# Where the split weight tiles of a two-layer encoder start inside their SBUF buffers

## The chip, the cores and the metric

One Trainium2 chip; the program runs on one of its cores. The metric is device microseconds of one execution of the whole program, and the time of a kernel is the median of several executions. One further execution is taken with the profiler on, and all rows below come from that one.

## What is computed

Two transformer layers on 256 tokens of width 1024, in float32. Each layer is a SwiGLU block, a mixer with three attention branches that share one input projection, and a second SwiGLU block. Cut to what matters here:

```python
for l in range(DEPTH):                                   # DEPTH = 2, D_MODEL = 1024, D_FF = 2816
    x = x + 0.5 * swiglu(rmsnorm(x, norm_ffn1[l]), w_ffn1_in[l], w_ffn1_out[l])
    h = rmsnorm(x, norm_mix[l])
    qa, ka, va, qb_, kb, vb, qc, kc, vc, gate_logits = jnp.split(h @ w_in[l], split_points, axis=-1)
    y_a, y_b, y_c = mixer_a(...), mixer_b(...), mixer_c(...)
    branches = jnp.einsum('bsnw,nwd->bsnd', jnp.stack([y_a, y_b, y_c], axis=2), w_branch[l])
    gates = jax.nn.sigmoid(gate_logits.reshape(b, s, N_BRANCH, D_MODEL))
    x = x + jnp.sum(gates * branches, axis=2) @ w_out[l]
    x = x + 0.5 * swiglu(rmsnorm(x, norm_ffn2[l]), w_ffn2_in[l], w_ffn2_out[l])
return rmsnorm(x, norm_final)
```

The weights are 215 MB in float32 and each is read once.

## The kernel before

Every weight matrix is cut into chunks of one MB, 2048 float32 in each of 128 partitions, and all chunks stand in one list, `specs`, in the order of use (196 of them). `ahead` keeps the list moving: it issues the load of a chunk to a `raw` buffer from SP, and `split` makes two tiles of it. The **upper part** `hi` is the chunk rounded to the type fp32r (L284, a cast on ScalarE), the **lower part** `lo` is the rest, raw minus hi (L285, a subtraction on VectorE, or on GpSimd for 25 chunks). Each of the two instructions covers half a chunk, 1024 elements. `raw`, `hi` and `lo` have a pool each with three buffers (`wraw`, `whi`, `wlo`), so the chunks take buffers 0, 1, 2, 0, 1, 2 in turn.

Activations are split in the same way. A product is then three matmuls into one PSUM bank, by `mm3` (L301 to L303): upper weights by upper activations, upper weights by lower activations, lower weights by upper activations. In `mm3` a 128x128 piece of `hi` or `lo` is the stationary operand, loaded anew for each matmul, and 256 tokens of the activations are the moving one. TensorE is written by hand and runs these loads and matmuls in program order, so that a stage is a long run of pairs of one load and one matmul. The names in the rows are those of the PSUM tiles that are written:

- `gu`: the gate and up projections of a SwiGLU block, moving operand `xgh`, `xgl` (the normalised input, 8 slices of 256 tokens), 4224 matmuls in four blocks.
- `fm`: the mixers' input projections, the same moving operand, 1920 matmuls.
- `facc`: the SwiGLU output projection of three of the four blocks, moving operand `hh`, `hl`, 1584 matmuls.
- `br`: the three branch projections of the mixers, moving operand `yah` to `ycl`, 576 matmuls.
- `wacc`: the mixers' output projection, moving operand `mh`, `ml`, 384 matmuls.

Two places use the weights as moving operand, 512 wide: `facc` of the last block (L382 to L384, 264 matmuls) and `vps`, the attention values (L874 to L876, 96 matmuls). The rest of TensorE's work (`sc`, `pt`, `o`, `oc` and small ones, attention) does not touch `hi` or `lo`.

The tiles' places in SBUF are fixed when the program is built. Before the change all three `hi` buffers and all three `lo` buffers start at the same place in a span of 512 bytes: byte 256 (their addresses are 69376, 77568, 85760 and 93952, 102144, 110336). A 128-column piece of weights is 512 bytes long and starts at a multiple of 512 bytes in its tile, so that every stationary operand starts at byte 256 of such a span too. The moving operands of `facc`, `br` and `wacc` also start at byte 256; those of `gu` and `fm`, `xgh` and `xgl`, start at byte 448.

Of the kernel before, what the change touches and what calls it, by code (L numbers as in the profile page):

```python
# [12 lines left out]
F32R = mybir.dt.float32r  # L13
# [4 lines left out]
P = 128  # L18
# [53 lines left out]
def encoder(ctx: ExitStack, tc: tile.TileContext, a, rope, onehot, out):  # L72
# [3 lines left out]
    whi = ctx.enter_context(tc.tile_pool(name="whi", bufs=3))  # L76
    wlo = ctx.enter_context(tc.tile_pool(name="wlo", bufs=3))
# [10 lines left out]
    def f(ap):  # L88
        return ap.bitcast(F32)
# [171 lines left out]
    raws, parts = [], []  # L261

    def ahead(n_raw, n_split):
        while len(raws) < min(n_raw, len(specs)):
            srcs, shape, _ = specs[len(raws)]
            raw = wraw.tile([P] + shape, F32, tag="raw", name="raw")
            for sl, ap in srcs:
                nc.sync.dma_start(out=raw if sl is None else raw[sl], in_=ap)
            raws.append(raw)
        while len(parts) < min(n_split, len(specs)):  # L270
            for _ in split(2):
                pass

    def split(n, eng=None):

        _, shape, pool_lo = specs[len(parts)]
        raw = raws[len(parts)]
        hi = whi.tile([P] + shape, F32R, tag="hi", name="hi")
        lo = wlo.tile([P] + shape, F32R, tag="lo", name="lo")
        parts.append((hi, lo))  # L280
        n = shape[0] // n
        for i in range(0, shape[0], n):
            h = slice(i, i + n)
            nc.scalar.copy(out=hi[:, h], in_=raw[:, h])  # L284
            (eng or (nc.gpsimd if pool_lo else nc.vector)).tensor_sub(lo[:, h], raw[:, h], f(hi[:, h]))  # L285
            yield
# [648 lines left out]
    with tc.manual_schedule(engines=BY_HAND):  # L935
        gains(rows, 2 * KT, 0)
        sst = sm.tile([P, 2], F32, name="sst", bufs=1)
        state["sst1"] = sm.tile([P, 2], F32, name="sst1", bufs=1)
        xps = [bank(acc, "ps_x") for _ in range(4)]
        for tt in range(2):  # L940
            for m in range(KT):
                nc.tensor.transpose(xps[m // 2][:, m % 2, cs(tt)], xtok[:, tt, cs(m)], ident)
        first = split(4, nc.gpsimd)
        for b in range(4):
            for i in range(2):
                m = 2 * b + i
                nc.scalar.activation(out=xgh[:, m, :], in_=xps[b][:, i, :], func=AF.Identity, scale=gcol[:, m:m + 1])
            nc.vector.tensor_copy(out=xT[:, 2 * b:2 * b + 2, :], in_=xps[b])
            for i in range(2):
                scaled_lo(2 * b + i, 0)  # L950
            next(first)
        for _ in first:
            pass
        for tt in range(2):
            for i in range(2):
                junk = t2("junk").rearrange("p a s -> p (a s)")
                acc_to = sst if i == 0 else state["sst1"]
                nc.scalar.activation(out=junk, in_=xtok[:, tt, i * 512:(i + 1) * 512], func=AF.Square, accum_out=acc_to[:, tt:tt + 1])
        nc.vector.tensor_add(sst, sst, state["sst1"])
        state["sst"] = sst  # L960
# [36 lines left out]
```

## Time and profile before

| | |
|---|---|
| median of 3 executions | 1248.13 us (1247.22 to 1248.27) |
| profiled execution | 1248.98 us, of which the span from the first to the last instruction is 1247.2 us |
| TensorE, matmuls | 1199.9 us busy, 96% of the span, 9720 matmuls |
| TensorE, weight loads | 1175.2 us, 94%, 9720 loads |
| VectorE, ScalarE, GpSimd | 812.0, 679.4 and 391.5 us busy (65%, 54%, 31%) |
| mean granted clock of TensorE | 0.987 of full speed |

How to read it: a matmul's row lasts some 280 ns, but the next one starts some 115 ns after it, since they are pipelined and their ends are modelled. What a stretch of TensorE costs is therefore read from the starts of its matmuls, or from their count in a stretch that is busy throughout, not from the duration of one. [...]

### The profile page before, as it was taken

To read this page: it belongs to the slowest core of one execution; us is meant where nothing else is said; L and a number is where in the kernel's file an instruction comes from. 1 tells how busy PE (TensorE), PEld (TensorE's weight loads), DVE (VectorE), ACT (ScalarE), POOL (GpSimd) and SP (SyncE) were. 2 spreads that over 40 slices of the span, in tenths; PEclk is the share of its full clock that TensorE was granted. 3 is DMA by queue.
4 is the path that set the end of the run, shared out by engine and by line. 5 is a ranking of instruction groups with operands and counts; after the bars stand their busy time and mean duration, and the time that the engine had idled before them with its cause. 6 is when DMAs were issued, how large, how long until landed. Compare 5 with 4: busy or idle time off the path is not lost. (4 is left out here: it accounts for less than half of the span.)

```text
span 1247.2 us, 23166 instructions
## 1 busy us (share of the span) xinstructions
PE 1199.9 (96%) x9720; PEld 1175.2 (94%) x9720; DVE 812.0 (65%) x1090; ACT 679.4 (54%) x1117; POOL 391.5 (31%) x244
## 2 busy tenths in 40 slices
PE   7999999998999999999999999998999999999997
PEld 6999999898999999999999999987988999999996
DVE  5565557777778675555575555587688867655554
ACT  5444445488875564434463443455988665444443
POOL 2221215643343232222242222274443613222221
PEclk9999999999999999999999999998999999999999
DMA  7658664344445456655555555544444445555550
GB/s 255 208 200 289 211 200 148 124 160 132 133 154 177 152 189 200 198 176 200 178 195 182 191 197 178 191 137 142 137 154 151 136 168 170 204 171 198 175 200 34
DMA packets 169365, 218.16 MB, mean 175 GB/s; under 512 B 4302, under 2 KB 147200, under 8 KB 169260
## 3 DMA queue, kind: packets, MB, share of 16 engines
q1 hardware_dynamic: 168652, 215.09, 51.8%
q8 instruction: 76, 1.25, 0.4%
q10 hardware_dynamic: 464, 1.06, 0.2%
q0 software_dynamic: 144, 0.52, 0.1%
q14 instruction: 29, 0.24, 0.1%
HBM read 215.59 MB, written 4.22 MB: 176 GB/s over the span
## 5 line engine op out<-in xcount | busy, mean ns | idle before, releaser
L284 ACT CAST hi<-raw 128x1024 fp32r<-128x1024 f32 (+1 forms) x394 | 399.1, 1043 | 413.4 <-issue 356.2
L285 DVE TENSOR_TENSOR lo<-raw,hi 128x1024 fp32r<-128x1024 f32 x342 | 455.1, 1357 | 134.0 <-ACT hi L284 133.2
L302 PE MATMUL gu<-xgl,hi 128*128 128x256 f32 x1408 | 393.1, 279 | 4.8 <-DVE xgl L316 4.8
L301 PE MATMUL gu<-xgh,hi 128*128 128x256 f32 x1408 | 393.6, 280 | 0.2 <-ACT hi L284 0.2
L303 PE MATMUL gu<-xgh,lo 128*128 128x256 f32 x1408 | 391.8, 278 | 0.0
L302 PEld LDWEIGHTS gu<-xgl,hi 128*128 128x128 f32 x1408 | 265.9, 189 | 6.3 <-DVE xgl L316 5.1
L301 PEld LDWEIGHTS gu<-xgh,hi 128*128 128x128 f32 x1408 | 265.8, 189 | 1.8 <-ACT hi L284 1.4
L303 PEld LDWEIGHTS gu<-xgh,lo 128*128 128x128 f32 x1408 | 267.1, 190 | 0.0
L475 POOL TENSOR_TENSOR gr<-gr,R 128x512 f32<-128x512 f32 x44 | 84.5, 1921 | 406.3 <-ACT gr L474 406.3
L302 PE MATMUL fm<-xgl,hi 128*128 128x256 f32 x640 | 183.8, 287 | 4.2 <-DVE xgl L316 4.2
L301 PE MATMUL fm<-xgh,hi 128*128 128x256 f32 x640 | 185.2, 289 | 0.0
L303 PE MATMUL fm<-xgh,lo 128*128 128x256 f32 x640 | 183.2, 286 | 0.0
L303 PE MATMUL facc<-hh,lo 128*128 128x256 f32 x528 | 149.3, 283 | 0.0
L301 PE MATMUL facc<-hh,hi 128*128 128x256 f32 x528 | 149.2, 283 | 0.0
L302 PE MATMUL facc<-hl,hi 128*128 128x256 f32 x528 | 149.1, 282 | 0.0
L285 POOL TENSOR_TENSOR lo<-raw,hi 128x1024 fp32r<-128x1024 f32 (+1 forms) x52 | 123.4, 2385 | 79.5 <-ACT hi L284 79.5
L302 PEld LDWEIGHTS fm<-xgl,hi 128*128 128x128 f32 x640 | 126.2, 197 | 4.7 <-DVE xgl L316 4.6
L301 PEld LDWEIGHTS fm<-xgh,hi 128*128 128x128 f32 x640 | 126.5, 198 | 0.1
L303 PEld LDWEIGHTS fm<-xgh,lo 128*128 128x128 f32 x640 | 126.0, 197 | 0.0
L480 POOL TENSOR_TENSOR hl<-hid,hh 128x512 fp32r<-128x512 f32 x44 | 77.6, 1764 | 106.0 <-ACT hh L479 106.0
L303 PEld LDWEIGHTS facc<-hh,lo 128*128 128x128 f32 x528 | 101.0, 191 | 0.0
L302 PEld LDWEIGHTS facc<-hl,hi 128*128 128x128 f32 x528 | 101.0, 191 | 0.0
(223 smaller groups left out, 1827.1 us busy)
## 6 DMA issues: line engine op xcount, KB each, us to landing
raw<-in_w_ffn_in_dram SPq DMA_DIRECT2D x87, 1024.0 KB, 4.9
raw<-in_w_ffn_out_dram SPq DMA_DIRECT2D x44, 1024.0 KB, 4.9
raw<-in_w_in_dram SPq DMA_DIRECT2D x38, 1024.0 KB, 5.0
raw<-in_w_branch_dram SPq DMA_DIRECT2D x12, 1024.0 KB, 5.2
raw<-in_w_out_dram SPq DMA_DIRECT2D x8, 1024.0 KB, 4.8
G<-skew SPq DMA_DIRECT2D x24, 192.0 KB, 3.7
raw<-in_w_in_dram SPq DMA_DIRECT2D x8, 512.0 KB, 5.0
skew<-vec_d SPq DMA_DIRECT2D x6, 512.0 KB, 7.3
```

What stands on the lines that cost most here:

```text
L284: nc.scalar.copy(out=hi[:, h], in_=raw[:, h])
L285: (eng or (nc.gpsimd if pool_lo else nc.vector)).tensor_sub(lo[:, h], raw[:, h], f(hi[:, h]))
L301: nc.tensor.matmul(ps, lhsT=hi[:, k, sl], rhs=xh, start=st, stop=False, **chk)
L302: nc.tensor.matmul(ps, lhsT=hi[:, k, sl], rhs=xl, start=False, stop=False, **chk)
L303: nc.tensor.matmul(ps, lhsT=lo[:, k, sl], rhs=xh, start=False, stop=last, **chk)
L475: nc.gpsimd.tensor_mul(gr, gr, Rb)
L480: nc.gpsimd.tensor_sub(hl, hid, f(hh))
```

## The change

The `hi` and `lo` tiles are allocated 16 float32 longer than the chunk (8256 bytes in each partition for 8192), and what the rest of the kernel sees as the tile is a view into it that starts at element `off`. For chunk number c of the list, `off` is 2 * (c // 3 % 8): 0, 2, 4 to 14 elements, which is 0, 8, 16 to 56 bytes. Three chunks in a row, one for each buffer, have the same offset, and after 24 chunks the offsets repeat. `hi` and `lo` of a chunk have the same one.

```diff
-        hi = whi.tile([P] + shape, F32R, tag="hi", name="hi")
-        lo = wlo.tile([P] + shape, F32R, tag="lo", name="lo")
+
+        n_el, off = shape[0] * shape[1], 2 * (len(parts) // 3 % 8)
+        hi, lo = (pool.tile([P, n_el + 16], F32R, tag=t, name=t)[:, off:off + n_el].rearrange("p (a b) -> p a b", a=shape[0]) for pool, t in ((whi, "hi"), (wlo, "lo")))
         parts.append((hi, lo))
```

The program that is built has the same instructions in the same order on every engine, with the same waits. What differs in it is the start address of operands. Of the 9048 matmuls that read `hi` or `lo`, 7800 read them at a place that is not a multiple of 64 bytes. And since each buffer is 64 bytes longer, the tiles behind it move: the `hi` buffers now start at bytes 256, 320 and 384 of a span of 512 bytes, the `lo` buffers at 448, 0 and 64 (the offset comes on top), and all tiles that are allocated behind them, among them the moving operands of `facc`, `br` and `wacc`, move from byte 256 to byte 128. `xgh` and `xgl` lie ahead of them and stay at byte 448.

## Rows read from the trace of the kernel before

**Rows 1.** The page's line on the engines: busy time, share of the span, instructions.

```profile
PE 1199.9 (96%) x9720; PEld 1175.2 (94%) x9720; DVE 812.0 (65%) x1090; ACT 679.4 (54%) x1117; POOL 391.5 (31%) x244
```

**Rows 2.** Busy time by stage: us, each engine's busy time (instructions), clock, DMA share, GB/s.

```profile
205.00:440.00 235.00, 220.42 (x1743) 215.30 (x1743) 179.16 (x306) 160.62 (x323) 95.33 (x55) 0.96 0.46 153
440.00:628.00 188.00, 188.00 (x1617) 187.66 (x1616) 113.57 (x116) 87.81 (x113) 49.58 (x33) 1.00 0.56 187
```

**Rows 3.** Matmul groups: line, tiles, shapes, count | busy us, mean ns | idle before, releaser.

```profile
L301 PE MATMUL gu<-xgh,hi 128*128 128x256 f32 x1408 | 393.6, 280 | 0.2 <-ACT hi L284 0.2
...
L301 PE MATMUL fm<-xgh,hi 128*128 128x256 f32 x640 | 185.2, 289 | 0.0
...
L301 PE MATMUL facc<-hh,hi 128*128 128x256 f32 x528 | 149.2, 283 | 0.0
...
L301 PE MATMUL wacc<-mh,hi 128*128 128x256 f32 x128 | 36.2, 283 | 0.0
...
L384 PE MATMUL facc<-hi,hl 128*128 128x512 f32 x88 | 34.3, 389 | 0.0
...
L303 PE MATMUL br<-yah,lo 128*128 128x256 f32 x64 | 18.1, 283 | 0.0
```

**Rows 4.** TensorE in steady stretches: us, busy (matmuls begun or running), clock, DMA, GB/s.

```profile
62.00:72.00 10.00, 10.00 (x91) 1.00 0.60 208
1218.00:1228.00 10.00, 10.00 (x87) 1.00 0.01 2
320.50:322.50 2.00, 2.00 (x20) 1.00 0.85 325
337.00:341.00 4.00, 4.00 (x37) 1.00 0.07 26
109.00:112.00 3.00, 3.00 (x27) 1.00 1.00 343
421.00:443.00 22.00, 22.00 (x186) 1.00 0.54 181
987.00:989.00 2.00, 2.00 (x19) 1.00 0.04 8
1077.00:1082.00 5.00, 5.00 (x25) 1.00 0.60 210
841.00:848.00 7.00, 7.00 (x33) 1.00 0.50 172
```

**Rows 5.** Timeline, first and last matmul of 62 to 72 us: start us, us, instruction.

```profile
62.01 0.28 PE L302 MATMUL gu<-xgl,hi 128*128 128x256 f32 x1
...
71.98 0.28 PE L303 MATMUL gu<-xgh,lo 128*128 128x256 f32 x1
```

**Rows 6.** Timeline, first and last matmul of 1218 to 1228 us.

```profile
1218.06 0.28 PE L301 MATMUL gu<-xgh,hi 128*128 128x256 f32 x1
...
1227.95 0.28 PE L301 MATMUL gu<-xgh,hi 128*128 128x256 f32 x1
```

**Rows 7.** Timeline, first and last matmul of 421 to 443 us.

```profile
421.08 0.28 PE L303 MATMUL wacc<-mh,lo 128*128 128x256 f32 x1
...
442.93 0.28 PE L302 MATMUL wacc<-ml,hi 128*128 128x256 f32 x1
```

**Rows 8.** Weight loads by group: count | busy us, mean ns | idle before.

```profile
L303 PEld LDWEIGHTS gu<-xgh,lo 128*128 128x128 f32 x1408 | 267.1, 190 | 0.0
...
L301 PEld LDWEIGHTS wacc<-mh,hi 128*128 128x128 f32 x128 | 24.6, 192 | 0.0
```

**Rows 9.** The split of the chunks on VectorE, ScalarE and GpSimd, by group.

```profile
L285 DVE TENSOR_TENSOR lo<-raw,hi 128x1024 fp32r<-128x1024 f32 x342 | 455.1, 1357 | 134.0 <-ACT hi L284 133.2
L284 ACT CAST hi<-raw 128x1024 fp32r<-128x1024 f32 x390 | 396.5, 1047 | 413.4 <-issue 356.2 <-PE gu L302 21.6 <-PE fm L302 16.8
...
L285 POOL TENSOR_TENSOR lo<-raw,hi 128x1024 fp32r<-128x1024 f32 x48 | 118.4, 2478 | 72.1 <-ACT hi L284 72.1
```

## The prediction

> **What bounds the kernel now.** First the page's line on the engines: TensorE is busy 96% of the span, no other engine over 65% [rows 1]. Then the stages: in the SwiGLU stretch from 440 to 628 us TensorE is busy for all 188 us, and in the mixer from 205 to 440 us for 220 of 235 [rows 2]. So the time is the sum of TensorE's steps, and every nanosecond by which a matmul follows the last one later reaches the end. The change touches the stationary operand of 4224 gu, 1920 fm, 1584 facc, 576 br and 384 wacc matmuls: three lines each, so three times the counts 1408, 640, 528 and 128 of the groups, and nine groups of 64 for br [rows 3]. That is 8688 in all; 1 ns more or less per matmul is 8.7 us, or 0.7% of the time. 0.2%, about what a measurement of this kernel can tell from no change, is 2.5 us: 0.29 ns per matmul.
>
> The third thing to see is that equal pairs of a 128-column load and a 256-column matmul do not go at one pace. In a gu stretch of the first block, 88 steps lie between the starts at 62.01 and 71.98 us, 113.3 ns each [rows 5]. In the last block it is 84 steps between 1218.06 and 1227.95 us: 117.7 ns [rows 6]. In wacc it is 182 steps between 421.08 and 442.93 us: 120.0 ns [rows 7]. The counts in stretches without a gap say the same (a row lasts 0.28 us, so those begun 0.28 us before a stretch are in its count) [rows 4]: gu 10.28/91 = 113 ns and 10.28/87 = 118 ns, fm 2.28/20 = 114 and 4.28/37 = 116, facc, wacc and br 3.28/27, 22.28/186 and 2.28/19, all 120 to 121. The clock was full in all of them, and VectorE, ScalarE and DMA were busy in fast and slow ones alike. facc, br and wacc have 120 wherever they run; gu and fm have 113.3 or 117.8 and keep it for a whole stretch. Of their 5946 starts that follow one another within 130 ns, 3891 come after at most 114 ns and 1926 after 115 to 119: a mean of 114.9. Loads in wacc's stretches take 192 ns, in gu's 190 [rows 8].
>
> What sets the two kinds apart? Not the shapes, nor the PSUM bank: br adds up in one bank over many matmuls as gu does, and has 120. It is the place of the operands. In facc, br and wacc stationary and moving operand start at the same byte (256) of a span of 512; in gu and fm the moving one starts 192 bytes further on. I take from this that load and matmul, which read SBUF at the same time, get in each other's way by an amount that hangs on where the two streams stand to each other. The change alters just that.
>
> [...]
>
> **The change part by part.** It adds and removes no instruction, and moves none; all it can do is alter the duration of steps.
>
> *The matmuls at 120 ns*, 1584 + 576 + 384 = 2544. Their operands no longer start at the same byte: the moving one is at 128, the six weight buffers at 256, 320, 384, 448, 0 and 64 plus 0 to 56. So differences of all sizes occur, and none stays at zero. Bounds: all stay at 120.0 (0 us), or all fall to 113.3 (2544 x 6.7 = -17.0 us). I take the middle, 116.7, since the rows show both paces for differences that are not zero, and no rule which: -2544 x 3.3 = **-8.4 us**.
>
> *The matmuls at 114.9 ns on average*, 4224 + 1920 = 6144. Their difference was 192 for every load. It now goes over the whole span, and for one lo buffer, at 448 as xgh is, it comes near zero: the relation of the slow kind. Bounds: all at 113.3 (-9.8 us), or all at 120.0 (+31.3 us). I take the same middle, 116.7, because after the change the two kinds have alike mixtures of differences: 6144 x 1.8 = **+11.1 us**.
>
> *The 360 wide matmuls*, where the weights are the moving operand. In the last block's facc 5.39 us hold 25 of them (a row lasts 0.39), 216 to 227 ns each, in vps 7.39/33 = 224 [rows 4]; on the timeline 226.7 and 229.3. One kind taking the other's pace is at most 264 x 2.6 = 0.7 us up or 0.2 down. I take **+0.3 us**.
>
> *The split itself.* 390 casts of 1047 ns, 342 subtractions of 1357 and 48 of 2478 now write, and the subtractions also read, at odd places [rows 9]. No row shows such an instruction off its place, so by the rows it could cost or gain something; TensorE's own spread of 6% between places is the nearest. Six percent of a cast is 63 ns and of a subtraction 81 ns, 25 and 28 us of busy time in all. I take nothing for it, as ScalarE waits 356 us for nothing but its turn before casts, and VectorE 134 us for casts [rows 9]; this cover is gone only in the mixers, where VectorE is busy 179 and ScalarE 161 of 235 us [rows 2]. A third of the chunks are there, so at worst some 8 us of each, of which the 15 us of TensorE's idle time per mixer would let through a part: 0 to 4 us, and the same downwards.
>
> Sum: -8.4 + 11.1 + 0.3 = **+3.0 us**. On the profiled execution's 1248.98 us that is 1252.0; the median of the runs is 0.85 us lower, within their spread, so I leave it at **1252**. The mean pace after the change is the term that decides. I give it 1.4 ns to either side of the middle (115.3 to 118.1), a fifth of the way between the ends: 12 us, so this case alone ranges from 1240 to 1264.
>
> **The rivals.**
>
> *Nothing hangs on the weights' place.* 113.3 and 120 may come from the place of the moving operand alone, or from how a stretch was entered: gu has two paces with one and the same pair of places, which a rule on the difference alone doesn't explain. Against it: wacc, facc and br move to another place too, by 384 bytes. Time: 1249, within 2 us.
>
> *Faster: the collisions go.* If only equal starting bytes make 120 ns, the 2544 slow pairs fall to 113.3 and gu and fm stay as they are: -17.0 us, 1232; with half of it, 1240. The place is facc, br and wacc; it decides as long as gu and fm lose less than 17.0/6144 = 2.8 ns each. For it: every one of these pairs has the same byte today, and every one is slow. Against it: gu's own stretches at 117.8 show a loss at an unequal place.
>
> *A load that starts off its place reads one piece more.* 7488 of the 8688 pieces of weights now do so. The only amounts by which the rows show a pair late are 4.4 and 6.7 ns (117.7 and 120.0 against 113.3); if half the off-place loads pay the smaller, it is +16 us, 1265, if all pay the larger, +50 us, 1299; middle 1280. For it: TensorE's loads are busy 94% of the span [rows 1], so a longer load has no room beside the matmul. Against it: nothing in this trace starts off its place, so no row shows such a price.
>
> [...]
>
> **How the numbers follow.** Paces mix, 1252: 45%. Nothing hangs on it, 1249: 25%. Collisions go, 1232 to 1240: 15%. One piece more, 1265 to 1299: 15%. Of the first, a bit over half lies above 1250.6, a fifth within 2.5 us of today, a quarter below. So slower by over 0.2%: 0.25 + 0.15 = 0.40; the same: 0.25 + 0.09 = 0.34; faster: 0.15 + 0.11 = 0.26. Both signs are in it; the likeliest case's own range is 1240 to 1264. The range for 8 in 10 leaves out the lower half of the third case and the upper half of the fourth: 1236 to 1282.
>
> **What would show it.** In the timeline after the change: facc, br and wacc no longer at 120.0 throughout but between 113 and 120, differing by chunk; gu and fm with a pace that changes from chunk to chunk, and steps of 120 in the chunks whose lo stands near xgh. If the pace follows the offset and not the buffer, with chunks of offset 0 (every 24th to 26th) the fastest, the third rival is right. If facc is at 120.0 and gu at 113.3 and 117.8 as before, the first is. Means of the split's rows off 1047, 1357 and 2478 by over 1% would say that the split feels it. A mean pace outside 113 to 120 would make the forecast wrong.

## The result and the profile after

The changed kernel takes 1255.24 us (median of 3 executions, 1254.3 to 1259.18) against 1248.13: a ratio of 1.0067, with a 95% interval of 1.0053 to 1.0081. It is slower by 7.1 us; the forecast, 1252, lies 3 us below it. The profiled execution is that of 1254.3 us, with a span of 1252.5; before, 1248.98 and 1247.2.

The page's line on the engines, which answers [rows 1]:

```profile
PE 1209.3 (97%) x9720; PEld 1182.3 (94%) x9720; DVE 805.4 (64%) x1090; ACT 679.4 (54%) x1117; POOL 380.7 (30%) x244
```

The same 9720 matmuls are busy for 9 us more, while GpSimd is busy for 11 us less and VectorE for 7, each with as many instructions as before. GpSimd's share was in no step of the forecast.

Next TensorE in stretches without a gap, as in [rows 4]; columns are the stretch, busy time (matmuls begun or running), granted clock (1.00 is full speed), DMA share, GB/s. They are gu of the first block, gu of the last, facc, wacc and br:

```profile
62.00:73.00 11.00, 11.00 (x95) 1.00 0.60 200
1223.00:1233.00 10.00, 10.00 (x88) 1.00 0.01 2
74.00:78.00 4.00, 4.00 (x36) 1.00 0.49 171
419.50:441.00 21.50, 21.50 (x183) 1.00 0.56 191
985.00:989.50 4.50, 4.50 (x40) 1.00 0.85 287
```

Read as before (a row lasts 0.28 us, so 0.28 goes on top): 11.28/95 = 119 ns, 10.28/88 = 117, 4.28/36 = 119, 21.78/183 = 119, 4.78/40 = 120, each to within one matmul of the count. The two kinds have become one. From all starts that follow each other at full clock:

| mean pace, ns | gu | fm | facc | br | wacc | wide facc | vps |
|---|---|---|---|---|---|---|---|
| before | 114.6 | 115.7 | 119.7 | 119.9 | 120.0 | 226.9 | 229.3 |
| after | 118.3 | 118.3 | 118.4 | 118.5 | 118.5 | 231.8 | 233.0 |

The split of the chunks, as in [rows 9] (mean duration in the last column ahead of the second bar):

```profile
L286 DVE TENSOR_TENSOR lo<-raw,hi 128x1024 fp32r<-128x1024 f32 x342 | 454.7, 1356 | 128.4 <-ACT hi L285 127.5
L285 ACT CAST hi<-raw 128x1024 fp32r<-128x1024 f32 x390 | 396.1, 1046 | 423.3 <-issue 370.0 <-PE gu L303 22.1 <-PE fm L303 13.2
...
L286 POOL TENSOR_TENSOR lo<-raw,hi 128x1024 fp32r<-128x1024 f32 x48 | 107.8, 2258 | 72.0 <-ACT hi L285 72.0
```

VectorE's subtractions and ScalarE's casts do not feel the change (1356 for 1357, 1046 for 1047 ns). GpSimd's subtractions take 2258 ns where they took 2478.

**Where the time went.** The paces alone make 4224 x 3.7 + 1920 x 2.6 = +20.6 us for gu and fm, 1584 x -1.2 + 576 x -1.4 + 384 x -1.5 = -3.3 for facc, br and wacc, 264 x 4.9 + 96 x 3.7 = +1.6 for the wide ones: +18.9 us. The span grew by 5.3. The rest was given back, and the five stages say where. First the kernel before, then the one after: the first SwiGLU block, mixer, two SwiGLU blocks, mixer, last block, each from its first matmul to that of the next. Columns: stretch, its length, then busy time (instructions) of TensorE, its loads, VectorE, ScalarE and GpSimd, granted clock, DMA share, GB/s.

```profile
8.68:201.75 193.07, 188.27 (x1589) 186.90 (x1590) 115.59 (x126) 90.80 (x118) 47.01 (x30) 1.00 0.66 219
201.75:443.17 241.42, 226.84 (x1799) 221.72 (x1798) 185.58 (x318) 166.92 (x338) 100.37 (x60) 0.96 0.45 150
443.17:813.20 370.03, 370.03 (x3183) 369.35 (x3181) 221.00 (x217) 168.51 (x210) 95.75 (x61) 1.00 0.57 188
813.20:1053.24 240.04, 224.15 (x1798) 218.51 (x1797) 180.90 (x315) 166.07 (x337) 100.99 (x61) 0.98 0.45 150
1053.24:1247.20 193.96, 186.46 (x1344) 175.36 (x1342) 108.47 (x112) 84.46 (x114) 46.72 (x30) 0.99 0.49 163
```

```profile
8.97:205.28 196.31, 191.29 (x1590) 190.00 (x1591) 115.63 (x126) 90.61 (x118) 46.91 (x30) 0.98 0.65 215
205.28:441.60 236.32, 223.49 (x1798) 217.42 (x1797) 181.40 (x319) 167.07 (x339) 95.14 (x60) 0.99 0.47 153
441.60:819.51 377.91, 377.91 (x3183) 377.34 (x3182) 220.95 (x217) 168.30 (x210) 95.60 (x61) 1.00 0.55 184
819.51:1055.80 236.29, 223.53 (x1798) 217.43 (x1797) 178.28 (x315) 166.16 (x337) 95.52 (x61) 0.99 0.46 152
1055.80:1252.50 196.70, 189.13 (x1344) 176.84 (x1342) 108.60 (x113) 84.54 (x115) 46.87 (x30) 0.99 0.48 161
```

In the two SwiGLU blocks in the middle TensorE has not one gap, before or after, and the slower pace arrives whole: +7.9 us. The first and the last block become longer by 3.2 and 2.7. But the two mixers are shorter by 5.1 and 3.8 us, although the 960 matmuls of fm in each became slower by 2.6 ns and those of br and wacc faster by only 1.4 and 1.5: +3.6 us over both. GpSimd is busy there for 5 us less in each, VectorE for 4.2 and 2.6, and the mean granted clock is 0.99 instead of 0.96 and 0.98: over both mixers it stood at 0.50, the lower of the two levels in these two traces (1.00 and 0.50), for 6.8 us, where it had for 27.3.

### The profile page after: what moved, and what is told of

The parts are those of the page before. It is cut to its first block, busy times and chain, and to the rows that moved or that the text cites. A ratio compares the mean times of both kernels' runs of the same rounds, so it can differ in the third digit from the quotient of the medians.

```text
span 1252.5 us, 23166 instructions
## 1 busy us (share of the span) xinstructions
PE 1209.3 (97%) x9720; PEld 1182.3 (94%) x9720; DVE 805.4 (64%) x1090; ACT 679.4 (54%) x1117; POOL 380.7 (30%) x244
## 5 line engine op out<-in xcount | busy, mean ns | idle before, releaser
L286 DVE TENSOR_TENSOR lo<-raw,hi 128x1024 fp32r<-128x1024 f32 x342 | 454.7, 1356 | 128.4 <-ACT hi L285 127.5
L303 PE MATMUL gu<-xgl,hi 128*128 128x256 f32 x1408 | 397.5, 282 | 5.0 <-DVE xgl L317 5.0
L304 PE MATMUL gu<-xgh,lo 128*128 128x256 f32 x1408 | 395.8, 281 | 0.0
L302 PE MATMUL fm<-xgh,hi 128*128 128x256 f32 x640 | 182.1, 285 | 0.0
L286 POOL TENSOR_TENSOR lo<-raw,hi 128x1024 fp32r<-128x1024 f32 (+1 forms) x52 | 112.9, 2183 | 79.7 <-ACT hi L285 79.7
L303 PEld LDWEIGHTS fm<-xgl,hi 128*128 128x128 f32 x640 | 122.0, 191 | 4.6 <-DVE xgl L317 4.1
L302 PEld LDWEIGHTS fm<-xgh,hi 128*128 128x128 f32 x640 | 122.1, 191 | 0.1
L304 PEld LDWEIGHTS fm<-xgh,lo 128*128 128x128 f32 x640 | 121.9, 190 | 0.0
L302 PEld LDWEIGHTS facc<-hh,hi 128*128 128x128 f32 x528 | 99.5, 188 | 0.0
```

The source lines that it names most:

```text
L302: nc.tensor.matmul(ps, lhsT=hi[:, k, sl], rhs=xh, start=st, stop=False, **chk)
L303: nc.tensor.matmul(ps, lhsT=hi[:, k, sl], rhs=xl, start=False, stop=False, **chk)
L304: nc.tensor.matmul(ps, lhsT=lo[:, k, sl], rhs=xh, start=False, stop=last, **chk)
```

## The experiments

All ran beside the kernel before, whose median was 1247.5 to 1248.1 us in each set. **Theory A**: what counts is where the load's stream of addresses stands to the matmul's. **Theory B**: a load that starts inside a piece of 64 bytes pays. **Theory C**: the moving operand's own place counts. Theories D and E came later, with the mixers.

### e1: the longer tiles alone

```diff
-        n_el, off = shape[0] * shape[1], 2 * (len(parts) // 3 % 8)
+        n_el, off = shape[0] * shape[1], 0
```

> The tiles are 16 elements longer, but every view starts at element 0: buffers at bytes 256, 320, 384 (hi) and 448, 0, 64 (lo) of 512, moving operands of facc, br and wacc at 128, no start inside 64 bytes. Theory A (what counts is where the load's stream stands to the matmul's, in steps of 64 bytes and more): the paces mix as in the changed kernel, gu and fm about 117.5 ns, facc, br and wacc about 118, time 1251 to 1256. Theory B (a load that starts inside a 64-byte piece pays): nothing pays here, gu 114.6, facc 119.7 as before, time 1248 within 2.

Measured: 1260.97 us (ratio 1.0113, 1.0096 to 1.0130); gu and fm 117.5 ns, facc, br and wacc 117.9. No operand starts inside 64 bytes, and yet the paces have mixed. So the 64 bytes by which the buffers are longer are enough for most of the change's effect on TensorE, without any offset. This speaks against B. The time is 5 to 10 us over what A expected, and over that of the change itself although the paces are lower: the mixers took 240.2 and 243.0 us, not 236.3. Something in the offsets makes the mixers shorter.

### e2: the offsets alone

Offsets as in the change, tiles 64 elements longer, so that buffers start at byte 0 or 256 of 512 and the moving operands stand as before the change.

```diff
-P, n_el + 16], F32R, tag=t, name=t)
+P, n_el + 64], F32R, tag=t, name=t)
```

> The offsets 0 to 56 bytes as in the change, but the tiles are 64 elements longer, so the buffers start at bytes 256 or 0 of 512 and the moving operands stay where they were before the change (256; xgh 448). Theory A: offsets under 64 bytes hardly move the streams, so facc, br and wacc stay within 1 ns of 120 and gu and fm within 1 ns of 115, time 1246 to 1252. Theory B: seven chunks of eight pay, all paces rise to those of the changed kernel, 118.3 or more, time 1254 to 1259.

Measured: 1254.29 us (ratio 1.0049, 1.0034 to 1.0064), gu 117.7, fm 117.1, facc 118.4. The offsets alone are enough too. By the mean B comes nearer than A; by chunk neither is right. Mean pace of gu and fm by how far the moving operand stands ahead of the weights, modulo 256 bytes, over triples of `mm3` at full clock:

| difference, bytes | 136 | 144 | 152 | 160 | 168 | 176 | 184 | 192 |
|---|---|---|---|---|---|---|---|---|
| offset of the chunk | 56 | 48 | 40 | 32 | 24 | 16 | 8 | 0 |
| ns | 118.6 | 119.8 | 118.6 | 117.8 | 114.6 | 118.7 | 118.4 | 114.5 |

Buffers at byte 0 and at byte 256 give the same (114.2 and 114.9 at 192; 114.4 and 115.0 at 168), so the relation repeats after 256 bytes. A start 24 bytes inside a piece of 64 costs nothing: B falls. But 8 bytes do matter (184: 118.4), so A's "steps of 64 bytes" falls with it. What stands is a relation that is fine to 8 bytes and has no order that I can see.

### e3 and e4: one side moved alone

e3 puts an unused tile of 48 float32 behind the `lo` pool, so that hh, mh and the y tiles stand 192 bytes further on; the weights and xgh stay. e4 puts it ahead of the `hi` pool, and another of 80 behind `lo`, so that only the weights move, to where xgh and xgl stand.

```diff
     wlo = ctx.enter_context(tc.tile_pool(name="wlo", bufs=3))
+    pada = ctx.enter_context(tc.tile_pool(name="pada", bufs=1))
+    pada.tile([P, 48], F32, name="pada")
```

> As before the change, but an unused tile of 192 bytes ahead of the small tiles moves the moving operands of facc, br and wacc from byte 256 to byte 448 of 512, where xgh stands; weights at 256. Theory A: facc, br and wacc get gu's paces, 113.3 or 117.8 ns instead of 120.0, 6 to 17 us off, time 1231 to 1243. Theory B and a theory by which PSUM or the order of the loop makes the 120 ns: 120.0 stays, time 1248 within 2.

> As before the change, but the weights alone stand 192 bytes further on, at byte 448 of 512, where xgh and xgl stand; all moving operands as before. Theory A: gu and fm now have the same byte on both sides and get 120.0 ns, +31 us less what the clock gives back, time 1265 to 1282; facc, br and wacc leave 120.0. Theory C (the moving operand's own place counts, 448 is fast and 256 slow): gu stays at 114.6 and facc at 119.7, time 1248 within 2. Theory B: no change either.

TensorE's stretches, e3 first: wacc, facc, gu. Then e4: gu, wacc. Last e3's two mixers, columns as for the five stages.

```profile
418.00:438.00 20.00, 20.00 (x179) 1.00 0.57 193
72.00:77.00 5.00, 5.00 (x46) 1.00 0.54 188
62.00:71.00 9.00, 9.00 (x82) 1.00 0.64 221
```

```profile
63.00:73.00 10.00, 10.00 (x85) 1.00 0.62 210
426.50:448.00 21.50, 21.50 (x185) 1.00 0.56 190
```

```profile
198.27:438.88 240.61, 223.56 (x1798) 218.28 (x1797) 184.78 (x318) 166.71 (x338) 100.29 (x59) 0.96 0.45 150
808.32:1047.77 239.45, 223.84 (x1799) 218.46 (x1798) 180.03 (x315) 165.48 (x337) 100.77 (x60) 0.96 0.45 150
```

With the moving operands 192 bytes ahead, wacc goes at 20.28/179 = 113.3 ns instead of 120.0, and facc at 115, mean 114.8. With the weights where xgh is, gu goes from 114.6 to 10.28/85 = 121, mean 119.9; fm 119.8; and wacc, now at a difference of 64, at 117.8. Theory C is out: xgh was not moved in e4. Both pure shifts did to the pace what A said, and e4 did it to the time: 1271.58 us (ratio 1.0189, 1.0174 to 1.0205). e3's time did not follow: 1246.12 us over 10 executions from 1240.5 to 1249.5 (0.9985, 0.9969 to 1.0001), and 1242.6 in the profiled one, where the pace alone should have given 13 us. Its mixers took 240.6 and 239.4 us with matmuls 0.6 to 6.7 ns faster: TensorE was idle there for 2.2 us more than before (length less busy time), and the granted clock stood at 0.50 for 34.1 us instead of 27.3. So in the mixers a faster TensorE waits; their length is set by something else.

e3 also shows that the two places are not all that counts. In the two middle SwiGLU blocks 1062 of gu's 2072 steps took 115 to 119 ns, where 261 did before, though neither of gu's operands had moved; most of what facc gained there was lost by this, and the stage took 369.4 us for 370.0.

### e5: no offsets of 8 bytes

In the changed kernel GpSimd's subtraction takes 1999 to 2151 ns on average at offsets 8, 24, 40 and 56, and 2446 to 2641 at 0, 16, 32 and 48. **Theory D**: this makes the mixers shorter. **Theory E**: slower matmuls fill TensorE's waits there.

```diff
-        n_el, off = shape[0] * shape[1], 2 * (len(parts) // 3 % 8)
+        n_el, off = shape[0] * shape[1], 4 * (len(parts) // 3 % 4)
```

> The change with offsets 0, 16, 32, 48 bytes only, same tile length. In the changed kernel GpSimd's 26 subtractions at offsets 8, 24, 40, 56 take about 2000 to 2150 ns and the 22 at 0, 16, 32, 48 about 2430 to 2640. Theory D (it is this that made the changed kernel's mixers 9 us shorter): GpSimd's mean is back at 2450 to 2510, the mixers take 240 to 243 us each, paces 117.5 to 118.5 as in the changed kernel, time 1259 to 1264. Rival E (the mixers are shorter because the matmuls are slower and so wait less): mixers 236 to 237 us, time 1254 to 1257.

GpSimd's group, and the first mixer:

```profile
L286 POOL TENSOR_TENSOR lo<-raw,hi 128x1024 fp32r<-128x1024 f32 x48 | 119.1, 2495 | 71.1 <-ACT hi L285 71.1
205.69:445.56 239.87, 222.95 (x1799) 216.89 (x1798) 185.90 (x319) 166.76 (x339) 100.71 (x60) 0.99 0.45 151
```

Measured: 1261.92 us (ratio 1.0116, 1.0103 to 1.0129), paces 118.0 and 118.3, mixers 239.9 and 241.1. The paces are those of the change, the mixers those of before: D, not E. The granted clock alone is not it either: in e5's first mixer it is 0.99 as in the change's, and that mixer is 3.5 us longer.

### e6: raw moved instead

hi, lo and the moving operands keep their relation of before; `raw` starts 8 bytes into its buffer.

```diff
-            raw = wraw.tile([P] + shape, F32, tag="raw", name="raw")
+            n_el = shape[0] * shape[1]
+            raw = wraw.tile([P, n_el + 16], F32, tag="raw", name="raw")[:, 2:2 + n_el].rearrange("p (a b) -> p a b", a=shape[0])
```

> Kernel before with the raw tiles' view 8 bytes into their buffers; hi, lo and all moving operands stand to each other as before the change. Theory D with a relation (raw and hi 8 bytes apart in 16): GpSimd's subtraction 2000 to 2050 ns in all 48, mixers 235 to 238 us, paces 114.6 and 119.7 as before, time 1238 to 1243. Theory D with the own place of hi or lo: GpSimd 2478 as before, time 1248 within 2. Rival E: 1248 within 2.

GpSimd's group, and the stages mixer, SwiGLU, mixer:

```profile
L288 POOL TENSOR_TENSOR lo<-raw,hi 128x1024 fp32r<-128x1024 f32 x48 | 99.5, 2082 | 78.6 <-ACT hi L287 78.6
```

```profile
202.76:438.86 236.10, 223.68 (x1799) 218.09 (x1797) 178.49 (x318) 167.26 (x338) 90.87 (x60) 0.98 0.46 153
438.86:808.87 370.01, 370.01 (x3182) 369.35 (x3181) 220.91 (x217) 168.38 (x210) 95.76 (x61) 1.00 0.57 188
808.87:1046.14 237.27, 224.03 (x1798) 218.43 (x1797) 175.26 (x315) 166.29 (x337) 91.60 (x61) 0.98 0.45 152
```

Measured: 1240.55 us (ratio 0.9934, 0.9920 to 0.9948): faster by 0.7%. The SwiGLU stage is 370.0 us as before, the paces are 115.0 and 119.8; all of the gain lies in the mixers, 5.3 and 2.8 us. So the subtraction gets faster though neither hi nor lo has moved.

From GpSimd to TensorE this goes, at least in part, by VectorE. No row has TensorE waiting for a `lo` of GpSimd; of its idle time in the mixers 24.8 us before and 19.7 in e6 end with an instruction of VectorE. VectorE's instructions there, the same in number, are busy for 12.7 us less in e6 (185.58 and 180.90 before, 178.49 and 175.26 now). On the timeline, before and then in e6, GpSimd subtracts the two halves of a chunk, and two small instructions of VectorE begin meanwhile and end just after one half each:

```profile
240.46 4.68 POOL L285 TENSOR_TENSOR lo<-raw,hi 128x1024 fp32r<-128x1024 f32 x2
240.53 2.36 DVE L889 TENSOR_TENSOR sA<-sA,r_tok 128x20 f32<-128x20 f32 x1 [3.66 <-POOL sA L888]
242.92 2.26 DVE L890 TENSOR_SCALAR sA<-sA 128x16 f32<-128x16 f32 x1
```

```profile
239.12 3.96 POOL L288 TENSOR_TENSOR lo<-raw,hi 128x1024 fp32r<-128x1024 f32 x2
239.19 1.97 DVE L892 TENSOR_TENSOR sA<-sA,r_tok 128x20 f32<-128x20 f32 x1 [3.66 <-POOL sA L891]
241.19 1.92 DVE L893 TENSOR_SCALAR sA<-sA 128x16 f32<-128x16 f32 x1
```

So a subtraction of GpSimd can hold up an instruction of VectorE until it ends. The clearest group is `e<-e,ra` (256 elements): before the change it has a median of 482 ns, but of 2600 in the four cases that begin during such a subtraction. How much of the 8 us came this way was not tested.

### e9 and e10: which operand

Tiles of 64 more elements as in e2; in e9 only hi starts 8 bytes in, in e10 only lo.

```diff
+        hi, lo = (pool.tile([P, n_el + 64], F32R, tag=t, name=t)[:, o:o + n_el].rearrange("p (a b) -> p a b", a=shape[0]) for pool, t, o in ((whi, "hi", 2), (wlo, "lo", 0)))
```

> Only hi 8 bytes into its buffer, lo and raw at 0; buffers of hi and lo at bytes 0 or 256 of 512. If what slows GpSimd's subtraction is its two reads (raw and hi) at one place of 16 bytes: 2000 to 2090 ns. If it is a read against the write of lo: raw and lo agree, so 2400 or more. hi's loads stand 184 bytes from xgh modulo 256, where e2 had 118.3 ns, so gu and fm are at 116 to 119.

> Only lo 8 bytes into its buffer, hi and raw at 0. If the two reads count: 2400 to 2500 ns as before. If the write counts: 2000 to 2090. gu and fm 114 to 118.

GpSimd's group, e9 and then e10:

```profile
L285 POOL TENSOR_TENSOR lo<-raw,hi 128x1024 fp32r<-128x1024 f32 x48 | 99.5, 2082 | 76.8 <-ACT hi L284 76.7
```

```profile
L285 POOL TENSOR_TENSOR lo<-raw,hi 128x1024 fp32r<-128x1024 f32 x48 | 118.5, 2481 | 71.1 <-ACT hi L284 71.1
```

It is the inputs, raw and hi, that count: the subtraction is slow when both start at a multiple of 16 bytes (2478 ns before, 2481 in e10) and fast when one of them is 8 bytes off (2082 in e6 and e9); where lo is written doesn't matter. Whether it is their distance that counts, or any input off a multiple of 16, no run tells, since none has both 8 bytes off. e9 is also the second test of D against E: its matmuls are the slowest after e4's (118.7 ns) and its mixers still take 234.4 and 235.5 us, against 240.6 and 239.7 in e10 with faster ones (116.0 and 117.9). Times: 1255.13 us (1.0056, 1.0023 to 1.0090) and 1251.93 (1.0032, 1.0016 to 1.0048).

### e7 and e8: both gains together

e7 is e6 with e3's 192 bytes. e8 starts hi and lo at 24 bytes, with buffers at byte 0 or 256 and all moving operands at 448, so that every pair differs by 168 modulo 256, and raw and hi by 8 modulo 16. (Three groups of small tiles have two buffers instead of four, to make room; what this does by itself was not run.)

```diff
+    pada.tile([P, 48], F32, name="pada")
...
+        n_el, off = shape[0] * shape[1], 6
+        hi, lo = (pool.tile([P, n_el + 64], F32R, tag=t, name=t)[:, off:off + n_el].rearrange("p (a b) -> p a b", a=shape[0]) for pool, t in ((whi, "hi"), (wlo, "lo")))
```

> e6 and e3 together: raw 8 bytes in, moving operands of facc, br and wacc 192 bytes further on than the weights modulo 256. Theories A and D: GpSimd 2000 to 2050 ns, all paces 113.3 to 115, time 1230 to 1238. If GpSimd does not gain by raw's place: as e3, 1242 to 1249.

> hi and lo all 24 bytes into their buffers (which start at bytes 0 or 256 of 512), all moving operands at byte 448, so that every pair differs by 168 modulo 256, where e2's gu ran at 113.3 to 115. Theories A and D: paces of gu, fm, facc, br and wacc 113.3 to 115, GpSimd's subtraction 2000 to 2050 ns, time 1230 to 1238. Theory B (a start inside 64 bytes pays): paces over 117, time over 1250.

Of e8: the stretches of gu, facc, wacc and the last block's gu, GpSimd's group, and the five stages.

```profile
61.00:71.00 10.00, 10.00 (x91) 1.00 0.65 214
72.00:76.00 4.00, 4.00 (x38) 1.00 0.55 190
410.50:431.00 20.50, 20.50 (x183) 1.00 0.60 204
1193.50:1203.50 10.00, 10.00 (x88) 1.00 0.01 2
```

```profile
L287 POOL TENSOR_TENSOR lo<-raw,hi 128x1024 fp32r<-128x1024 f32 x48 | 99.5, 2081 | 76.5 <-ACT hi L286 72.8 <-DVE nb L605 3.6
```

```profile
9.06:197.75 188.69, 183.94 (x1589) 182.38 (x1590) 114.90 (x125) 90.34 (x117) 46.06 (x29) 1.00 0.66 223
197.75:431.69 233.94, 218.93 (x1798) 212.78 (x1797) 180.05 (x318) 166.94 (x338) 90.85 (x59) 0.99 0.46 155
431.69:794.31 362.62, 362.31 (x3182) 361.38 (x3181) 220.90 (x217) 168.34 (x210) 95.56 (x60) 1.00 0.57 192
794.31:1028.32 234.01, 219.22 (x1798) 213.17 (x1797) 175.04 (x315) 166.31 (x337) 91.59 (x60) 0.99 0.46 154
1028.32:1223.10 194.78, 187.04 (x1344) 174.25 (x1342) 108.67 (x113) 84.85 (x115) 46.95 (x30) 0.99 0.48 162
```

e8 takes 1224.96 us, a ratio of 0.9828 (0.9811 to 0.9845): 5 us under its expectation, 23 us faster than the kernel before and 30 faster than the change. facc and wacc go at 113.3 ns, gu at 114.0, fm and br at 114.5. The middle stage falls from 370.0 to 362.6 us, the mixers from 241.4 and 240.0 to 234 each. Only the last block is not better (194.8 for 194.0): its wide matmuls went from 226.9 to 232.9 ns. e7 takes 1231.94 us (0.9860, 0.9830 to 0.9890; six executions from 1222.1 to 1237.0). Against e3 its change is raw's 8 bytes: 14 us.

All together. The time is the median of the executions, all else is from the profiled one; mixers are first matmul to first matmul, and the last column is how long the granted clock stood at 0.50 in both of them:

| kernel | time, us | gu, fm ns | facc, br, wacc ns | GpSimd ns | mixers, us | clock 0.50, us |
|---|---|---|---|---|---|---|
| before | 1248.1 | 114.9 | 119.8 | 2478 | 241.4, 240.0 | 27.3 |
| after | 1255.2 | 118.3 | 118.4 | 2258 | 236.3, 236.3 | 6.8 |
| e1 longer | 1261.0 | 117.5 | 117.9 | 2505 | 240.2, 243.0 | 23.9 |
| e2 offsets | 1254.3 | 117.5 | 118.3 | 2245 | 236.1, 237.4 | 10.2 |
| e3 moving 192 | 1246.1 | 114.9 | 114.5 | 2477 | 240.6, 239.4 | 34.1 |
| e4 weights 192 | 1271.6 | 119.9 | 117.5 | 2502 | 241.5, 241.4 | 23.9 |
| e5 offsets of 16 | 1261.9 | 118.0 | 118.3 | 2495 | 239.9, 241.1 | 17.1 |
| e6 raw 8 | 1240.6 | 115.0 | 119.8 | 2082 | 236.1, 237.3 | 20.5 |
| e7 e3 and e6 | 1231.9 | 114.7 | 115.0 | 2082 | 236.2, 233.8 | 17.1 |
| e8 all at 168 | 1225.0 | 114.1 | 113.6 | 2081 | 233.9, 234.0 | 13.7 |
| e9 hi 8 | 1255.1 | 118.7 | 118.7 | 2082 | 234.4, 235.5 | 10.2 |
| e10 lo 8 | 1251.9 | 116.0 | 117.9 | 2481 | 240.6, 239.7 | 20.5 |

Every kernel with a slow subtraction has mixers of 239.4 to 243.0 us, every one with a faster one 233.8 to 237.4, whatever its matmuls do. The middle stage goes by the paces alone.

## Why the prediction was right, and where it was not

The sign, the range and the mechanism held: equal pairs of load and matmul have a pace that hangs on where their two streams stand to each other, the change mixes those places, and the fast kind, 2.4 times as many, loses more in sum than the slow kind gains. e3 and e4 show it by moving one side alone by 192 bytes: wacc goes from 120.0 to 113.3 ns, gu from 114.6 to 119.9. But that the number came out near is luck: two errors offset each other.

- **The common pace.** The sum took the middle of 113.3 and 120.0, 116.7; it is 118.4 (118.3 and 118.4 for the two kinds), just outside the 115.3 to 118.1 that the forecast gave it. The step that failed is the reason for the middle: a mixture of differences need not lie in the middle of the two that a trace happens to show. At 168 and 192 the pace is 113.3 to 115, at zero 120, at all others of the table of e2 between 117.8 and 119.8. The kernel before had its largest group on one of the few good places. The forecast's sign of steps of 120 ns where lo stands near xgh did not show: in the changed kernel gu and fm go at 118.3 ns in the chunks with that lo buffer, and at 118.0 and 118.6 with the other two. Per matmul the fast kind lost 3.4 ns and the slow one gained 1.3, where the forecast had 1.8 and 3.3. With the right pace the terms were +20.6 us for gu and fm (forecast +11.1), -3.3 for facc, br and wacc (forecast -8.4) and +1.6 for the wide matmuls (forecast +0.3).
- **The split at nothing.** The forecast bounded it by 4 us either way, from ScalarE's casts and VectorE's subtractions and TensorE's spread of 6%. Those two groups kept their durations. What failed is that GpSimd's 48 subtractions got no term: they became 17% faster at half of the offsets (2000 for 2400 ns), and the mixers became 8.9 us shorter though their matmuls became slower by 3.6 us in sum: worth some 12 us. All 24 chunks of these subtractions stand in the mixers. There TensorE's idle time fell from 30.5 to 25.6 us over both, and its time at a granted clock of 0.50 from 27.3 to 6.8 us. e5 and e6 show that the subtraction's speed is the cause of shorter mixers. What is not shown is why the clock gave back more in the change than in e6, where the idle time fell as far, but the time at 0.50 only to 20.5 us.
- **Every nanosecond reaches the end.** This first step of the forecast held in the SwiGLU stages (+7.9 us in the middle, where the paces make +8.2) and not in the mixers: in e3 their matmuls became faster by some 7 us in sum, and the mixers shorter by 1.4.
- **Nothing hangs on the weights' place** fell with the tables of paces. Its argument, that gu has two paces at one and the same difference, stays true and unexplained: e3's gu still has 113.3 and 117.8.
- **Collisions go, faster.** The pairs with equal bytes did leave 120.0, but by 1.2 to 1.5 ns. gu and fm lost 3.7 and 2.6, 3.4 on average, more than the 2.8 at which that rival ended.
- **One piece more per load** is refuted by e8: all weights start 24 bytes into a piece of 64, and the pace is 113.3 to 114.5.

What stays open: what in SBUF or in TensorE makes the relation, since the runs show paces and no cause; why one difference has two paces, held for a whole stretch; and why the last block's wide matmuls are faster at a difference of zero (226.9 ns before) than at those of the change (231.8) and of e8 (232.9). Nor is the difference of a pair the whole rule. In e1 hi and lo of a chunk stand at differences of their own, and with hi at 128 and lo at 192 gu and fm go at 116.0 ns, facc and wacc at 118.7; with hi at 0 and lo at 64 facc, br and wacc go at 116.0 to 116.5, where both at 0 made 119.7 to 120.0 (before).

## What to carry to other kernels

Where equal instructions have unequal paces, compare the addresses of their operands early: the place of one buffer against another, modulo 256 bytes, moved TensorE by 6% here (113.3 to 120.0 ns per matmul), and an input's start modulo 16 bytes moved GpSimd by 17% (2002 for 2402 ns). Padding a pool is then a knob that costs no instruction, but it moves everything allocated behind it, so set the places of all streams that run together, as e8 does, instead of varying them. And cost an edit stage by stage: a slower bound in one stage and a shorter wait in another can hide each other in the total.

## What the runs showed that was not expected

GpSimd's subtraction of 1024 float32 per partition has a median of 2002 ns when one of its two inputs starts 8 bytes off a multiple of 16 (e6 to e9), and of 2402 when both start at one (before); VectorE's same subtraction has a median of 1225 ns before and in the change, and ScalarE's cast 1047 in both. While GpSimd subtracts, small instructions of VectorE took as long as the subtraction: 2.36 us for 20 elements per partition before, 1.97 in e6. In TensorE a shift of 8 bytes of the stationary operand was worth 4 ns of 114 (e2, 192 to 184). And a faster TensorE got little of its gain in the mixers: e3, with matmuls faster than before by up to 6.7 ns, was idle there for 2.2 us more and at a granted clock of 0.50 for 34.1 us instead of 27.3, and its median gained 2 us of 13; with the subtraction made faster too, the gain was 16 us (e7).
